# An encoder block with sixteen experts: weight tiles of neighbouring rows, token features permuted in their store, column tiles that stream runs of 32, and embedding inputs loaded ahead of the weights

## The chip, the cores and the metric

The kernel runs on one core of a Trainium2 chip. The metric is device time in microseconds (us); lower is better. Several runs of the kernel before were timed, and one further execution was recorded by the profiler. Engines are named as the profile names them: PE is TensorE (matmuls; PEld its weight loads), DVE VectorE, ACT ScalarE, POOL GpSimd, and SP the engine that issues most DMAs.

## The reference

Two requests, 256 and 512 tokens of 1024 features, pass through one block with shared weights: a mixer (dilated attention beside a bidirectional state space model), then a mixture of 16 experts in which each expert picks its tokens, then a gate that mixes in an embedding of each token. Everything is float32. The part that matters here:

```
aff = softmax(h @ w_router)                    # h: normed tokens (t, 1024); 16 experts
gate, idx = top_k(aff.T, 2 * t // 16)          # 64 tokens of 512, 32 of 256, per expert
ye = (silu(xe @ w_gate) * (xe @ w_up)) @ w_down   # xe = h[idx]; per expert 1024 -> 2816 -> 1024
out = zeros.at[idx].add(ye * gate)             # added back to the tokens' rows
...
e = rmsnorm(pe @ w_ple)                        # pe: an embedding input of 256 per token
x + sigmoid(rmsnorm(x) @ w_pg) * e
```

Each expert sees 96 tokens in all and has 34.6 MB of weights (w_gate and w_up 1024 x 2816, w_down 2816 x 1024), each of which is used once.

## The kernel before, in words

Up to the experts the block is worked off in a mixer part (projections, attention, state space), an output projection (`units_out`), and a router per 128 tokens (`router`, L770 on). The router squares and sums its rows, stores the updated rows to DRAM (`acc_d`, L782), scales the rows by the norm's gains on POOL (L786) and by the rstd on ACT (L787), and stores them to DRAM as `hn_d` (L788). `hn_d` and `acc_d` are laid out with four rows of 256 features for each token, its quarters j = 0 to 3. Then `top_k` finds each expert's tokens.

**Expert stage.** The 96 tokens are three blocks (b) of 32. `gather` (L1110 on) fetches for each block 128 rows of `hn_d`, so that partition 32j + token holds quarter j of that token. `turn_x` (L1116) turns such a block of 128 x 256 in squares of 32 x 32 on DVE, so that partition 32j + c has feature c of a group of 32 of quarter j, and the 32 tokens lie along the columns: a stationary operand of 128 x 32 for each of 8 contraction steps k. `blocks` (L1131) then runs, for each weight tile, 12 matmuls: for each block of tokens four column tiles j of 32 tokens, whose outputs go to partitions 32j to 32j + 31 of one PSUM bank. Column tile j streams a quarter of the weight tile's columns.

`up(e, r)` handles half r (1408) of the hidden features: 8 contraction steps, a gate tile and an up tile each; then ACT takes the silu, DVE the product and again a turn by squares of 32, which gives the stationary operands of `down(e, r)` with its 11 contraction steps. `emit` scales by the gates and adds the rows to `acc_d` by an indirect DMA. The order of the work is up(e, 0), down(e − 1, 1), emit(e − 1), up(e, 1), down(e, 0).

**Which row of a weight lies on which partition** is free so long as it agrees with the stationary operand. Before, a tile is loaded by `strips` (L203): 16 strips of 8 rows each, whose starts lie 1024/16 = 64 rows apart for gate and up, 1408/16 = 88 rows apart for down. Step k takes rows 8k to 8k + 7 of every strip. So quarter j's features must stand in the order (k, strip in the quarter, row) rather than (strip, k, row): `turn_x` has ACT copy each gathered block into `xp` with such a view (L1120, `by_strip` and `blocks32`), and the DVE product of the hidden features reads the same kind of view (L1151).

**The weights' stream.** `Feed` (L122) holds the list of all 864 expert tiles and the 8 tiles of w_pg that follow them. It has 22 slots of 5632 bytes per partition: 9 in the pool `w_b` (N_B), opened when attention's buffers are given back, 8 in `w_c` (N_C), 5 in `w_d` (N_D), opened when the embedding part's pool `ple` is given back. A slot that a tile's matmuls have finished with is loaded with the next tile. All these loads are issued by SP (L147), in the order of the list, in one queue with the other stores and loads of SP.

**The embedding part** runs beside the output projection. `ple_turn` (L825) takes the six blocks of tokens one after the other: it loads the input `pe` (128 x 256, two buffers; L829), and at a later step has PE transpose it and splits it into two parts for three-term matmuls. The first step of `ple_turn` is taken just ahead of `wf.add(w_b, N_B)` (L1058, L1059), so one `pe` load stands ahead of the first weights on SP, and the other five behind them.

Of the kernel before, what the change touches and what calls it, by code (L numbers as in the profile page):

```python
# [10 lines left out]
F32 = mybir.dt.float32  # L11
# [4 lines left out]
AF = mybir.ActivationFunctionType  # L16
ALU = mybir.AluOpType
# [4 lines left out]
P = 128  # L22
D = 1024
KD = D // P
NT = 6
# [8 lines left out]
NB = 3  # L34
FR = FF // 2
FC = FR // 4
DC = D // 4
KF = FR // P
PLE = 256
# [125 lines left out]
def block_kernel(ctx, tc, x_prompt, x_sample, p_prompt, p_sample, rel_bias, g_mix, w_in, conv_w, conv_b, dt_bias,  # L165
                 a_log, d_skip, g_ssd, w_out, g_ffn, w_router, w_gate, w_up, w_down, g_pg, w_pg, w_ple, g_ple,
                 g_final, c_masks, c_table, c_rows, y_prompt, y_sample):
    nc, E = tc.nc, mybir.EngineType
    S, Q = Group(0), Group(1)

    def rows(prompt, sample, t):
        return prompt[t * P:(t + 1) * P, :] if t < 2 else sample[(t - 2) * P:(t - 1) * P, :]

    x_rows = lambda t: rows(x_prompt[0], x_sample[0], t)
    p_rows = lambda t: rows(p_prompt[0, 0], p_sample[0, 0], t)
    N_B, N_C, N_D, PLE_A = 9, 8, 5, 4
    y_rows = lambda t: rows(y_prompt[0], y_sample[0], t)

    def row_bcast(v, n):
# [2 lines left out]
    def pool(name, side):  # L182
        return tc.alloc_tile_pool(name=name, bufs=1, side=side, reuse_waits="tile")
# [16 lines left out]
    items.append((w_ple[0].rearrange("(k p) c -> p k c", p=P), 2, D))  # L200
    ws = Stream(nc, items)

    def strips(w, r0, step, c0, n):  # L203

        w = w[r0:, c0:c0 + n]
        return bass.AP(tensor=w.tensor, offset=w.offset, ap=[[step * w.ap[0][0], 16], [w.ap[0][0], 8], [1, n]])

    def ups(e, r):
        return [strips(w[0, e], 8 * k, D // 16, FR * r, FR) for k in range(KD) for w in (w_gate, w_up)]

    def downs(e, r):
        return [strips(w_down[0, e], FR * r + 8 * k, FR // 16, 0, D) for k in range(KF)]

    def by_strip(ap):

        return ap.rearrange("p (q k v) -> p k q v", q=4, v=8)

    def blocks32(ap):
        return ap.rearrange("p (k q v) -> p k q v", q=4, v=8)

    order = []
    for e in range(NE):
        for r in range(2):
            order += ups(e, r) + (downs(e - 1 + r, 1 - r) if e + r else [])
# [10 lines left out]
    def bank(tag, bufs):  # L235
        return psum.tile([P, 512], F32, tag=tag, bufs=bufs, name=tag)

    pA = lambda: bank("pA", 2)
    pB = lambda: bank("pB", 3)
    pT = lambda: bank("pT", 2)  # L240
    pO = lambda: bank("pO", 1)
# [27 lines left out]
    def rstd_of(p, ss, n, width):  # L269
        r = p.tile([P, n], F32, tag="rstd", bufs=3, name="rstd")  # L270
        nc.vector.tensor_scalar(r, ss, 1.0 / width, EPS, op0=ALU.mult, op1=ALU.add)
        nc.gpsimd.tensor_tensor(r, r, mhalf[:, :n], op=ALU.pow)
        return r

    def sumsq(p, src, scr):
        ss = p.tile([P, 1], F32, tag="ss", bufs=3, name="ss")
        nc.scalar.activation(scr, src, AF.Square, accum_out=ss)
        return ss

    def transposes(src, k0, k, n=P, bank=None):  # L280
        p = (bank or pT)()
        for j in range(k):
            nc.tensor.transpose(p[:, j * n:(j + 1) * n], src[:, (k0 + j) * P:(k0 + j + 1) * P], ident[:n, :n])  # L283
        return p[:, :k * n].rearrange("p (j q) -> p j q", j=k)

    def split_to(hi, lo, src):
        nc.scalar.activation(hi, src, AF.Copy)  # L287
        nc.vector.tensor_tensor(lo, src, hi, op=ALU.subtract)
# [487 lines left out]
    def router(g, t, xm):  # L776

        row = slice(t * P, (t + 1) * P)
        hn = fin.tile([P, D], F32, tag="hn", bufs=2, name="hn")
        r = rstd_of(wk, sumsq(wk, xm, hn), 1, D)  # L780
        xT = fin.tile([P, KD, P], F32, tag="xT", bufs=2, name="xT")
        nc.sync.dma_start(g.acc_rows[row, :], xm)  # L782
        for k0 in (0, 4):
            src = transposes(xm, k0, 4)
            nc.scalar.activation(xT[:, k0:k0 + 4, :], src, AF.Copy)
        nc.gpsimd.tensor_tensor(hn, xm, gff, op=ALU.mult)  # L786
        nc.scalar.activation(hn, hn, AF.Copy, scale=r)  # L787
        nc.sync.dma_start(g.hn_rows[row, :], hn)  # L788
        yield
        pr = pB()  # L790
        for k in range(KD):
            nc.tensor.matmul(pr[:, :NE], lhsT=xT[:, k, :], rhs=wr[:, k, :], start=k == 0, stop=k == KD - 1)
        st = wk.tile([P, 4], F32, tag="st3", bufs=2, name="st3")
        af = wk.tile([P, NE], F32, tag="af", bufs=2, name="af")
        nc.vector.tensor_reduce(st[:, 0:1], pr[:, :NE], axis=AX.X, op=ALU.max)
        nc.vector.tensor_scalar(st[:, 1:2], st[:, 0:1], r, -1.0, op0=ALU.mult, op1=ALU.mult)
        nc.scalar.activation(af, pr[:, :NE], AF.Exp, bias=st[:, 1:2], scale=r, accum_out=st[:, 2:3])
        nc.vector.reciprocal(st[:, 3:4], st[:, 2:3])
        nc.vector.tensor_scalar(af, af, st[:, 3:4], None, op0=ALU.mult)
        yield  # L800
        p = pO()
        nc.tensor.transpose(p[:NE, :P], af, ident)
        nc.vector.tensor_copy(affs[0][g.row:g.row + NE, t * P:(t + 1) * P], p[:NE, :P])
        g.routed += 1
        yield
# [17 lines left out]
    evs, pts = {}, {}  # L823

    def ple_turn():  # L825

        for t in PLE_ORDER:
            pe = pw.tile([P, PLE], F32, tag="pe", bufs=2, name="pe")
            nc.sync.dma_start(pe, p_rows(t))  # L829
            yield  # L830
            pts[t] = [pw.tile([P, 2, P], F32R, name=f"pe{x}{t}") for x in "hl"]
            split_to(*pts[t], transposes(pe, 0, 2))
            yield

    def ple():
# [215 lines left out]
    gff = fin.tile([P, D], F32, name="gff")  # L1051
    nc.sync.dma_start(gff, row_bcast(g_ffn[0], D))
    w_b = pool("w_b", "right")
    pw = pool("ple", "right")
    PLE_ORDER = (2, 3, 4, 5, 0, 1)
# [30 lines left out]
    p, p_q = pO(), pB()  # L1086
# [19 lines left out]
    exw = pool("experts", "left")  # L1106
    of = (S, S, Q)
    xgs, xts, hts_, acc, pend = {}, {}, {}, {}, {}
# [7 lines left out]
    def turn_x(e):  # L1116
        xts[e] = [exw.tile([P, DC], F32, tag=f"x{b}", bufs=2, name="xe") for b in range(NB)]
        for b in range(NB):
            xp = exw.tile([P, DC], F32, tag="xp", bufs=2, name="xp")
            nc.scalar.activation(blocks32(xp), by_strip(xgs[e][b]), AF.Copy)  # L1120
            nc.vector.transpose(xts[e][b], xp)

    gather(0)
    wf.add(w_c, N_C)
# [1 line left out]
    w_d = pool("w_d", "right")  # L1126
    wf.add(w_d, N_D)
    turn_x(0)


    def blocks(out, st, k, w, n, first, last):  # L1131


        for b in range(NB):
            for j in range(4):
                q = slice(32 * j, 32 * j + 32)
                nc.tensor.matmul(out[b][q], lhsT=st[b][:, 32 * k:32 * k + 32], rhs=w[:, n * j:n * (j + 1)],  # L1137
                                 start=first[b], stop=last, skip_group_check=True)

    def up(e, r):  # L1140
        pg, pu = [pB()[:, :FC] for _ in range(NB)], [x()[:, :FC] for x in (pT, pT, pO)]
        for k in range(KD):
            for p in (pg, pu):
                i, w = wf.get()
                blocks(p, xts[e], k, w, FC, [k == 0] * NB, k == KD - 1)
                wf.free(i)
        hts_[e, r] = [exw.tile([P, FR // 4], F32, tag=f"h{b}", bufs=2, name="ht") for b in range(NB)]
        for b in range(NB):
            sg, hv = (exw.tile([P, FC], F32, tag=x, bufs=2, name=x) for x in ("sg", "hv"))
            nc.scalar.activation(sg, pg[b], AF.Silu)  # L1150
            nc.vector.tensor_tensor(blocks32(hv), by_strip(sg), by_strip(pu[b]), op=ALU.mult)  # L1151
            nc.vector.transpose(hts_[e, r][b], hv)  # L1152

    def down(e, r, after=None):
        if r == 0:
            two, one = pA(), pA()
            acc[e] = [two[:, :DC], two[:, DC:], one[:, :DC]]
        h = hts_.pop((e, r))
        for k in range(KF):
            i, w = wf.get()  # L1160
            first = r + k == 0
            blocks(acc[e], h, k, w, DC, [first, False, first], r == 1 and k == KF - 1)
            wf.free(i)
            if after:
                after()
# [12 lines left out]
    for e in range(NE):  # L1178
        if e + 1 < NE:
            gather(e + 1)  # L1180
        if 1 <= e <= NT:
            ple_norm(e - 1)
        for r in range(2):
            up(e, r)
            if r == 0 and e + 1 < NE:
                turn_x(e + 1)
            if e + r:
                down(e - 1 + r, 1 - r)
                if r == 0:
                    emit(e - 1)  # L1190
# [4 lines left out]
    def halve():  # L1195

        if len(wg) < KD and wf.n_dma == len(wf.items) and len(wf.slots) > 1:
# [3 lines left out]
            wf.slots.append(wf.held.pop(len(wf.items) - KD + i)[1])  # L1201

    down(NE - 1, 1, halve)
    emit(NE - 1)

# [22 lines left out]
    for t in range(NT):  # L1228
        if t + 1 < NT:
            tail_prep(t + 1)  # L1230
        xt, et, xh, xl, r = xs5.pop(t)
        sg = wf.tile(keep[1][t % 2], D)
        for c in range(2):
            s_ = slice(c * 512, (c + 1) * 512)
            p = pA()
# [5 lines left out]
        r = rstd_of(wk, sumsq(wk, sg, q5.tile([P, D], BF16, tag="scr5", bufs=1, name="scr5")), 1, D)  # L1241
# [64 lines left out]
```

## Time and profile before

| What | us |
| --- | --- |
| Median of three runs | 2746.53 (2706.67 to 2758.66) |
| The profiled execution, its own time | 2726.49 |
| Its span in the profile | 2724.6 |
| First expert matmul starts | 518.4 |
| Last expert matmul ends | 2616.0 |
| From there to the end | 108.6 |
| DMA moved, over the span | 642.07 MB |

How to read it: the profile is of one execution, and sums of parts have to be compared with its 2724.6 us span, which is 1.9 us less than its own time. In a group's row stand its line, engine, operation and operands, the number of instructions, their busy time, the mean duration of one, and the idle time of the engine ahead of them with what ended it. A float32 matmul appears as two records. The four column tiles of 32 run beside each other, so the records of one weight tile overlap, and a tile's time is read from the starts of successive tiles.

### The profile page before, as it was taken

What the parts mean: (1) busy time and instruction counts of PE and PEld (TensorE: products, weight loads), DVE (VectorE), ACT (ScalarE), POOL (GpSimd) and SP (SyncE); (2) the same over time, 40 slices, a digit from 0 to 9 for tenths busy, and PEclk for the clock granted to TensorE, in tenths of its full rate; (3) what the DMA queues carried; (4) which work ended last, traced back from release to release, by engine and by line L of the source; (5) the groups of instructions that cost most, each with busy time, mean ns of one, the idle gap of its engine ahead of it and who ended that gap; (6) DMA issues with size and microseconds to landing.
All of it is one profiled execution on the core that took longest, in us unless ns stands there. A gap on an engine that the chain in (4) does not pass through costs nothing.

```text
span 2724.6 us, 52864 instructions
## 1 busy us (share of the span) xinstructions
PE 2072.3 (76%) x23968; PEld 1073.0 (39%) x23968; DVE 476.4 (17%) x1001; ACT 417.8 (15%) x816; POOL 288.3 (11%) x279
## 2 busy tenths in 40 slices
PE   7999996797677767677777676766666777676758
PEld 6989895542222222222222222222222223222336
DVE  6675672400000000000000000000000000000024
ACT  5676363300000000000000000000000000000023
POOL 0343422200000000000001010101010000000000
PEclk9999998899999999999999999999999999999989
DMA  7441526999999999999999999999999999999952
GB/s 243 138 111 48 173 74 192 242 249 272 267 284 266 279 253 288 249 283 274 269 271 286 251 268 248 283 251 255 251 258 251 266 259 285 247 281 247 288 146 78
DMA packets 181743, 642.07 MB, mean 236 GB/s; under 512 B 21805, under 2 KB 56037, under 8 KB 181518
## 3 DMA queue, kind: packets, MB, share of 16 engines
q1 hardware_dynamic: 168318, 620.85, 85.9%
q0 software_dynamic: 13200, 17.84, 3.3%
q8 instruction: 188, 3.08, 0.5%
q14 instruction: 37, 0.30, 0.0%
HBM read 618.13 MB, written 19.96 MB: 234 GB/s over the span
## 4 chain that ended last, share of the span: by engine, by line
issue 73%; PE 13%; DMA 6%; POOL 4%; ACT 3%; DVE 2%; SPq 0%; POOLq 0%; DVEq 0%; ACTq 0%
PE pA L265 3%; PE pA L266 3%; PE pA L267 3%; DMA acc_d<-ye,quart 2%; POOL acc_d L1171 2%; PE pO L704 1%; POOL xg L1113 1%; DMA xg<-hn_d,quart 1%; DMA pe<-in_p_sample 1%; PE pT L695 1%; ACT ws L96 1%; DMA hn_d<-hn 1%; DMA ws<-in_w_in 1%; DVE ws L97 1%; PE pT L283 1%
## 5 line engine op out<-in xcount | busy, mean ns | idle before, releaser
L1137 PE MATMUL pB<-wf,xe 128*32 128x352 f32 x6144 | 517.1, 465 | 213.8 <-DMA wf<-in_w_gate 199.6
L1137 PE MATMUL pA<-wf,ht 128*32 128x256 f32 x8448 | 528.1, 384 | 177.2 <-DMA wf<-in_w_down 175.4
L1137 PE MATMUL pT<-wf,xe 128*32 128x352 f32 x4096 | 364.4, 466 | 181.8 <-DMA wf<-in_w_up 181.3
L1137 PEld LDWEIGHTS pA<-wf,ht 128*32 128x32 f32 x8448 | 245.2, 109 | 462.2 <-DMA wf<-in_w_down 330.7
L1137 PEld LDWEIGHTS pB<-wf,xe 128*32 128x32 f32 x6144 | 183.6, 110 | 533.9 <-DMA wf<-in_w_gate 293.9
L1151 DVE TENSOR_TENSOR hv<-sg,pT 128x352 f32<-128x352 f32 x64 | 32.1, 502 | 1942.7 <-PE pT L1137 1921.6
L1150 ACT ACTIVATE sg<-pB 128x352 f32<-128x352 f32 x96 | 44.6, 464 | 1619.1 <-PE pB L1137 1547.1
L1137 PEld LDWEIGHTS pT<-wf,xe 128*32 128x32 f32 x4096 | 114.6, 109 | 423.5 <-DMA wf<-in_w_up 292.7
L1171 POOL DMA_INDIRECT acc_d<-ye,quart x48 | 76.4, 1591 | 1563.6 <-ACT ye L1170 1447.4
L1137 PE MATMUL pO<-wf,xe 128*32 128x352 f32 x2048 | 204.9, 459 | 0.0
L1137 PEld LDWEIGHTS pO<-wf,xe 128*32 128x32 f32 x2048 | 70.5, 110 | 82.9 <-issue 70.4
L1113 POOL DMA_INDIRECT xg<-hn_d,quart x48 | 47.8, 996 | 446.9 <-ACT xp L1120 423.8
L97 DVE TENSOR_TENSOR ws<-ws 128x2048 fp32r<-128x2048 f32 (+1 forms) x31 | 69.4, 2241 | 40.3 <-ACT ws L96 40.3
L1170 ACT ACTIVATE ye<-pA,gates 128x256 f32<-128x256 f32 x48 | 19.4, 472 | 320.4 <-PE pA L1137 320.4
L96 ACT ACTIVATE ws<-ws 128x2048 fp32r<-128x2048 f32 (+1 forms) x31 | 55.9, 1806 | 29.7 <-PE pA L266 16.3
L265 PE MATMUL pA<-h,ws 128*128 128x512 f32 (+1 forms) x136 | 54.1, 398 | 0.0
L266 PE MATMUL pA<-h,ws 128*128 128x512 f32 (+1 forms) x136 | 53.8, 396 | 0.0
L267 PE MATMUL pA<-h,ws 128*128 128x512 f32 (+1 forms) x136 | 53.7, 395 | 0.0
L1152 DVE STREAM_TRANSPOSE ht<-hv 128x352 f32<-128x352 f32 x96 | 47.0, 515 | 0.6
L265 PE MATMUL pA<-hq,ws 128*128 128x256 f32 (+1 forms) x136 | 40.9, 302 | 4.7 <-ACT ws L96 4.1
L267 PE MATMUL pA<-hq,ws 128*128 128x256 f32 (+1 forms) x136 | 40.2, 297 | 1.3 <-DVE ws L97 1.3
L265 PE MATMUL pA<-ws,mh 128*128 128x512 f32 x96 | 38.8, 404 | 1.9 <-ACT mh L287 1.9
(302 smaller groups left out, 2048.9 us busy)
## 6 DMA issues: line engine op xcount, KB each, us to landing
wf<-in_w_gate SPq DMA_DIRECT2D x256, 704.0 KB
wf<-in_w_up SPq DMA_DIRECT2D x256, 704.0 KB
wf<-in_w_down SPq DMA_DIRECT2D x352, 512.0 KB
ws<-in_w_in SPq DMA_DIRECT2D x24, 1024.0 KB
tbl_rep<-tbl SPq DMA_DIRECT2D x8, 512.0 KB
ws<-in_w_out SPq DMA_DIRECT2D x4, 1024.0 KB
wf<-in_w_pg SPq DMA_DIRECT2D x8, 512.0 KB
sk<-tbl_rep SPq DMA_DIRECT2D x8, 448.0 KB
```

Source lines behind the costliest of these rows:

```text
L96: self.nc.scalar.activation(hi, raw, AF.Copy)
L97: self.nc.vector.tensor_tensor(lo, raw, hi, op=ALU.subtract)
L265: nc.tensor.matmul(out, lhsT=sh, rhs=mh, start=first, stop=False)
L266: nc.tensor.matmul(out, lhsT=sh, rhs=ml, start=False, stop=False)
L267: nc.tensor.matmul(out, lhsT=sl, rhs=mh, start=False, stop=last)
L283: nc.tensor.transpose(p[:, j * n:(j + 1) * n], src[:, (k0 + j) * P:(k0 + j + 1) * P], ident[:n, :n])
L1113: nc.gpsimd.indirect_dma_start(out=xgs[e][b], out_offset=None, in_=of[b].hn_d, in_offset=bass.IndirectOffsetOnAxis(ap=quart[:, b, e:e + 1] ...
L1137: nc.tensor.matmul(out[b][q], lhsT=st[b][:, 32 * k:32 * k + 32], rhs=w[:, n * j:n * (j + 1)], start=first[b], stop=last, skip_group_check= ...
L1150: nc.scalar.activation(sg, pg[b], AF.Silu)
L1151: nc.vector.tensor_tensor(blocks32(hv), by_strip(sg), by_strip(pu[b]), op=ALU.mult)
L1152: nc.vector.transpose(hts_[e, r][b], hv)
L1171: nc.gpsimd.indirect_dma_start(out=of[b].acc_d, out_offset=bass.IndirectOffsetOnAxis(ap=quart[:, b, e:e + 1], axis=0), in_=ye, in_offset=N ...
```

## The change

Three things are changed together.

1. *Rows that neighbour.* A weight tile is now 128 rows that follow each other. `strips`, `by_strip` and `blocks32` are gone.
2. *The orders that go with it.* Contraction step k of `up` needs features 128k + 32j + c on partition 32j + c. The router's POOL product therefore writes `hn` permuted, quarter j made of the 32-feature runs j of every 128 (`by_tile`), and `turn_x` turns the gathered block at once, without the ACT copy. Column tile j of a gate or up tile streams the runs j of 32 columns of every 128 (11 runs of 32 instead of 352 columns in a row), so that after the turn the hidden features stand in the order in which w_down's rows lie; the DVE product reads and writes in a row. Column tiles of w_down still stream 256 columns in a row.
3. *Embedding inputs.* All six `pe` loads are issued at the first step of `ple_turn`, each to a buffer of its own; the transposes follow in later steps. The pool `ple` is larger for that, and N_B, N_C, N_D are 8, 8, 6 instead of 9, 8, 5.

```
-    N_B, N_C, N_D, PLE_A = 9, 8, 5, 4
+    N_B, N_C, N_D, PLE_A = 8, 8, 6, 4
...
     def ups(e, r):
-        return [strips(w[0, e], 8 * k, D // 16, FR * r, FR) for k in range(KD) for w in (w_gate, w_up)]
+        return [w[0, e, P * k:P * (k + 1), FR * r:FR * (r + 1)] for k in range(KD) for w in (w_gate, w_up)]
 
     def downs(e, r):
-        return [strips(w_down[0, e], FR * r + 8 * k, FR // 16, 0, D) for k in range(KF)]
+        return [w_down[0, e, FR * r + P * k:FR * r + P * (k + 1), :] for k in range(KF)]
...
+    def by_tile(ap):
+
+        return ap.rearrange("p (k j c) -> p j k c", j=4, c=32)
...
-        nc.gpsimd.tensor_tensor(hn, xm, gff, op=ALU.mult)
+        nc.gpsimd.tensor_tensor(hn.rearrange("p (j k c) -> p j k c", j=4, c=32), by_tile(xm), by_tile(gff), op=ALU.mult)
...
+        pes = [pw.tile([P, PLE], F32, name=f"pe{t}") for t in range(NT)]
         for t in PLE_ORDER:
-            pe = pw.tile([P, PLE], F32, tag="pe", bufs=2, name="pe")
-            nc.sync.dma_start(pe, p_rows(t))
-            yield
+            nc.sync.dma_start(pes[t], p_rows(t))
+        yield
+        for t in PLE_ORDER:
             pts[t] = [pw.tile([P, 2, P], F32R, name=f"pe{x}{t}") for x in "hl"]
-            split_to(*pts[t], transposes(pe, 0, 2))
+            split_to(*pts[t], transposes(pes[t], 0, 2))
             yield
...
-            xp = exw.tile([P, DC], F32, tag="xp", bufs=2, name="xp")
-            nc.scalar.activation(blocks32(xp), by_strip(xgs[e][b]), AF.Copy)
-            nc.vector.transpose(xts[e][b], xp)
+            nc.vector.transpose(xts[e][b], xgs[e][b])
...
-                q = slice(32 * j, 32 * j + 32)
-                nc.tensor.matmul(out[b][q], lhsT=st[b][:, 32 * k:32 * k + 32], rhs=w[:, n * j:n * (j + 1)],
+                nc.tensor.matmul(out[b][32 * j:32 * j + 32], lhsT=st[b][:, 32 * k:32 * k + 32], rhs=w[:, j],
...
-                blocks(p, xts[e], k, w, FC, [k == 0] * NB, k == KD - 1)
+                blocks([x.rearrange("p (k c) -> p k c", c=32) for x in p], xts[e], k, by_tile(w), [k == 0] * NB, k == KD - 1)
...
-            nc.vector.tensor_tensor(blocks32(hv), by_strip(sg), by_strip(pu[b]), op=ALU.mult)
+            nc.vector.tensor_tensor(hv, sg, pu[b], op=ALU.mult)
...
-            blocks(acc[e], h, k, w, DC, [first, False, first], r == 1 and k == KF - 1)
+            blocks(acc[e], h, k, w.rearrange("p (j c) -> p j c", j=4), [first, False, first], r == 1 and k == KF - 1)
```

What moves on SP, at the place where the weights' stream begins (`pe` are the embedding inputs, `wf` the weight slots, `gff` the router's gains, `acc_d` and `hn_d` the router's stores). Before:

```order
L1052 DMA gff<-in_g_ffn 128x1024
L829 DMA pe<-in_p_sample 128x256
L147 DMA wf<-in_w_gate 128x1x1408
L147 DMA wf<-in_w_up 128x1x1408
...
L147 DMA wf<-in_w_gate 128x1x1408
L829 DMA pe<-in_p_sample 128x256 x2
L1176 DMA g<-in_g_ple 128x1024
L782 DMA acc_d_85<-xm 128x1024 x2
L788 DMA hn_d_84<-hn 128x1024 x2
L829 DMA pe<-in_p_sample 128x256
L829 DMA pe<-in_p_prompt 128x256 x2
```

and with the change:

```order
L1045 DMA gff<-in_g_ffn 128x1024
L821 DMA pe_4234<-in_p_sample 128x256
L821 DMA pe_4235<-in_p_sample 128x256
...
L821 DMA pe_4233<-in_p_prompt 128x256
L147 DMA wf<-in_w_gate 128x1408
L147 DMA wf<-in_w_up 128x1408
...
L147 DMA wf<-in_w_up 128x1408
L1166 DMA g<-in_g_ple 128x1024
L774 DMA acc_d_85<-xm 128x1024
L780 DMA hn_d_84<-hn 128x1024
```

Five `pe` loads have moved from behind the nine weight tiles of `w_b` to ahead of its eight. On ACT, where the expert stage begins, before:

```order
L277 ACTIVATE scr,ss<-ev 128x1024 x6
L1120 ACTIVATE xp<-xg 128x256 x8
L1150 ACT_TABLE_LOAD
L1150 ACTIVATE sg<-pB 128x352 x6
L1120 ACTIVATE xp<-xg 128x256 x3
L1150 ACTIVATE sg<-pB 128x352 x3
```

and with the change:

```order
L1140 ACTIVATE sg<-pB 128x352 x9
L1160 ACTIVATE ye<-pA,gates 128x256 x3
L1140 ACTIVATE sg<-pB 128x352 x6
```

The copies of gathered blocks (`xg` to `xp`) are gone; the silu steps (`sg`) follow each other, with only the scaling of the outputs (`ye`) between them.

More of the change, by code (lines that the diff above doesn't have):

```diff
@@ L201, in block_kernel @@
     ws = Stream(nc, items)
-    def strips(w, r0, step, c0, n):
-        w = w[r0:, c0:c0 + n]
-        return bass.AP(tensor=w.tensor, offset=w.offset, ap=[[step * w.ap[0][0], 16], [w.ap[0][0], 8], [1, n]])
     def ups(e, r):
-        return [strips(w[0, e], 8 * k, D // 16, FR * r, FR) for k in range(KD) for w in (w_gate, w_up)]
+        return [w[0, e, P * k:P * (k + 1), FR * r:FR * (r + 1)] for k in range(KD) for w in (w_gate, w_up)]
     def downs(e, r):
-        return [strips(w_down[0, e], FR * r + 8 * k, FR // 16, 0, D) for k in range(KF)]
[L214 to L219, printed above, removed]
+        return [w_down[0, e, FR * r + P * k:FR * r + P * (k + 1), :] for k in range(KF)]
+    def by_tile(ap):
+        return ap.rearrange("p (k j c) -> p j k c", j=4, c=32)
     order = []
@@ L1128, in block_kernel, with blocks @@
     turn_x(0)
-    def blocks(out, st, k, w, n, first, last):
+    def blocks(out, st, k, w, first, last):
         for b in range(NB):
             for j in range(4):
-                q = slice(32 * j, 32 * j + 32)
-                nc.tensor.matmul(out[b][q], lhsT=st[b][:, 32 * k:32 * k + 32], rhs=w[:, n * j:n * (j + 1)],
+                nc.tensor.matmul(out[b][32 * j:32 * j + 32], lhsT=st[b][:, 32 * k:32 * k + 32], rhs=w[:, j],
                                  start=first[b], stop=last, skip_group_check=True)
     def up(e, r):
-        pg, pu = [pB()[:, :FC] for _ in range(NB)], [x()[:, :FC] for x in (pT, pT, pO)]
+        pg, pu = ([x()[:, :FC] for x in xs] for xs in ((pB, pB, pB), (pT, pT, pO)))
         for k in range(KD):
```

## The prediction

> **What bounds the kernel now.** I read the windows by stage first. Columns: stretch, length, then for each engine its busy time (x instructions), then TensorE's granted clock, the busy share of the 16 DMA engines, GB/s.
>
> ```profile
> 400.00:460.00 60.00, 39.97 (x237) 33.85 (x236) 16.73 (x37) 17.35 (x29) 8.71 (x6) 0.86 0.69 184
> 460.00:500.00 40.00, 38.90 (x236) 33.14 (x235) 23.96 (x70) 19.61 (x40) 8.70 (x6) 1.00 0.72 200
> ...
> 2616.00:2724.60 108.60, 75.15 (x340) 60.08 (x336) 50.17 (x74) 38.37 (x60) 11.76 (x15) 0.86 0.23 77
> ```
>
> and the stretch from the first expert matmul to the last:
>
> ```profile
> 518.35:2616.00 2097.65, 1538.40 (x20736) 608.34 (x20736) 104.42 (x240) 81.97 (x189) 114.95 (x90) 1.00 1.03 265
> ```
>
> The experts take 2097.65 of 2724.6 us. In that stretch TensorE is busy for 73%, at full clock; the DMA engines never rest (1.03), yet bring only 265 GB/s. What the profile's groups say of the idle time agrees:
>
> ```profile
> L1137 PE MATMUL pB<-wf,xe 128*32 128x352 f32 x6144 | 517.1, 465 | 213.8 <-DMA wf<-in_w_gate 199.6
> L1137 PE MATMUL pA<-wf,ht 128*32 128x256 f32 x8448 | 528.1, 384 | 177.2 <-DMA wf<-in_w_down 175.4
> L1137 PE MATMUL pT<-wf,xe 128*32 128x352 f32 x4096 | 364.4, 466 | 181.8 <-DMA wf<-in_w_up 181.3
> ```
>
> 556 us of waiting, all for weights. By the DMA issues each gate or up tile is 704.0 KB (512 of them), each down tile 512.0 KB (352): 553.65 MB, which at 265 GB/s is 2089 us. So the stage is its transfers, and its rate is the question. Next I looked for other loads in the same trace. The last eight tiles of this queue are w_pg's: 128 rows that lie one behind the other, 4 KB each. The DMA view from 2600 to 2630 us, in 40 slices of 0.75 us (share in tenths, then GB/s):
>
> ```profile
> DMA  9999899999999999998999975543432000000000
> GB/s 213 257 240 268 235 229 240 262 251 229 224 235 240 224 235 218 251 273 213 399 404 404 393 284 208 213 175 158 164 137 93 33 0 0 0 0 0 0 0 0
> ```
>
> Up to the 19th slice the strips of w_down come, in packets of the same 4 KB, at 213 to 273 GB/s. Then, with the engines as busy as before, 399, 404, 404: w_pg. (Afterwards some engines have finished and the share falls.) Same queue, same packet, same destination, only other rows: the strips cost a third of the bandwidth. **I take 400 GB/s for rows that neighbour.**
>
> **Part 1, the experts' rows.** A strip tile reads 16 places, each 8 rows: 64 rows apart for gate and up (704 KB), 88 for down (352 KB). The new one reads 128 rows in a row; the bytes, packets' length, number of DMAs and their order stay. Before the matmuls begin, the 16 tiles of the first two pools can be loaded (11.5 MB); 542.1 MB remain: at 400 GB/s 1355 us. Beside them run the gathers and scatter-adds; in 1000 to 1140 us, about one expert, their queue took:
>
> ```profile
> q0 software_dynamic: 576, 0.79, 3.0%
> ```
>
> 3.0% of 140 us is 4.2 us per expert with the strips in the way; I take 3, so 48 us for 16. The stream then needs 1403 us.
>
> Now TensorE becomes the neighbour to watch. While tiles were in stock, its own pace shows in the timeline, one gate and one up tile (48 records) from row to row, and a run of 11 down tiles:
>
> ```profile
> 531.50 1.98 PE L1137 MATMUL pB<-wf,xe 128*32 128x352 f32 x24
> ...
> 535.05 1.98 PE L1137 MATMUL pB<-wf,xe 128*32 128x352 f32 x24
> ...
> 538.61 1.98 PE L1137 MATMUL pB<-wf,xe 128*32 128x352 f32 x24
> ...
> 577.65 0.42 PE L1137 MATMUL pA<-wf,ht 128*32 128x256 f32 x3
> ...
> 578.09 14.18 PE L1137 MATMUL pA<-wf,ht 128*32 128x256 f32 x256
> ```
>
> 7.11 us for two pairs: 1.777 us per gate or up tile (400 GB/s bring one in 1.80). Down: 264 records in about 14.4 us, 1.31 us per tile (1.31 by the DMA). An expert has 32 and 22: 56.9 + 28.8 = 85.7 us, 1371 us for 16. The two limits nearly meet; the stream is the longer by 32 us. Since neither covers the other's jitter, I add 13 us: **the stage takes 1416 us instead of 2098.**
>
> **Part 2, the strided moving operand.** A gate or up matmul now streams 11 runs of 32 columns, 128 apart, instead of 352 in a row; 8 blocks of 32 tokens and the PSUM side stay as they were. Time goes by columns: 1777 ns / 24 records / 352 columns is 0.210 ns, 1310 / 24 / 256 is 0.213, so nothing can be gained by it. What it could cost, the trace bounds only from afar: L494 streams runs of 8, L792 16 columns in a row.
>
> ```profile
> L792 PE MATMUL pB<-wr,xT 128*128 128x16 f32 x96 | 11.4, 256 | 0.2 <-ACT xT L785 0.2
> ...
> L499 PE MATMUL pB<-masks,ad 128*128 128x128 f32 x24 | 3.3, 274 | 0.0
> ...
> L494 PE MATMUL pB<-dt,masks 128*128 128x32 f32 x12 | 1.5, 274 | 0.0
> ```
>
> Runs of 8 take 274 ns, as 128 columns in a row do, and 7% over the shortest. So 0 to 7%; I take 0, since 32-column runs are nearer to a plain row. 7% would make an up tile 1.90 us and an expert 89.6, 1434 us in all, still inside the sum's slack. [...]
>
> **Part 3, the permuted store.** Six POOL products at L786 (2.4 us each) read permuted views. A POOL product with spread-out operands is L616, 1286 ns for 512 columns against 2400 for 1024:
>
> ```profile
> L786 POOL TENSOR_TENSOR hn<-xm,gff x6: 2340/2400/2411, 420.6 to 488.2; 128x1024 f32<-128x1024 f32 x6
> ```
>
> ```profile
> L616 POOL TENSOR_TENSOR w<-gt,dt 128x512 f32<-128x512 f32 x24 | 30.2, 1286 | 22.1 <-DVE gt L571 20.6 <-DVE e L619 1.6
> ```
>
> That is 0 to 0.2 us on the path, once; nothing in the sum. In return 48 ACT copies of 417 ns go; 47 lie under the weights' stream, where ACT is busy 4%, and one is ahead of the first expert matmul: −0.4 us. VectorE's products lose their strided reads; they too lie under the stream.
>
> **Part 4, the head.** Now only the first embedding tile is issued ahead of nine weights; TensorE's queue has the second one's transpose in front of other work and stands:
>
> ```profile
> 441.42 0.66 PE L283 MATMUL pT<-masks,pe 128*128 128x128 f32 x2 [17.86 <-DMA pe<-in_p_sample]
> ```
>
> With all six ahead of the weights this wait goes, −17.9 us. On SP's queue the six stand where the first one stood, behind its wait for the end of attention; the weights behind them waited for that before, too. [...]
>
> ```profile
> 492.35 14.91 DMA hn_d<-hn
> ...
> 508.02 16.55 DMA xg<-hn_d,quart x2
> ```
>
> ```profile
> 518.35 1.40 PE L1137 MATMUL pB<-wf,xe 128*32 128x352 f32 x8 [13.47 <-DVE xe L1121]
> ```
>
> The store stands behind weights on SP's queue: 14.91 x (1 − 265/400) = −5.0; a gather (9.1 us from issue to landing) by the same ratio −3. The six loads delay the weights by 0.79 MB, 2 to 3 us, hidden by the slack of 460 to 500 (share 0.72); of the 22 slots one opens later (w_b 8, w_d 6), hidden by the 16 tiles, 28 us of TensorE's work; without that cover, 1.8 us. The first expert matmul moves from 518.4 to **492.1**.
>
> **The sum**, for the profiled execution (2726.5 = 518.4 + 2097.6 + 108.6 + 1.9 outside the span): 492.1 + 1416 + 108.6 + 1.9 = 2019. The tail is not touched. The runs shown have their median 0.7% above the profiled one; I add 6 us for that: **2025 us**. Its own range is 1970 (TensorE alone sets the stage: 1371 + 603) to 2110 (375 GB/s: 1446 + 61 + 603).
>
> **Rivals.** (a) *The long rows don't reach 400.* w_pg's 512 KB lie in one piece; gate and up take halves of 11 KB rows, 64% of the bytes of an expert. Two stretches of ordinary loads while TensorE works, most of their packets 1 to 4 KB:
>
> ```profile
> 28.00:36.00 8.00, 6.74 (x59) 6.03 (x57) 5.82 (x8) 6.44 (x7) 0.00 (x0) 1.00 0.95 313
> 300.00:350.00 50.00, 49.39 (x227) 40.21 (x226) 23.98 (x49) 22.79 (x40) 21.03 (x27) 1.00 0.65 203
> ```
>
> 313 / 0.95 = 329 and 203 / 0.65 = 312 GB/s at full share; by the lower 492 + 1737 + 61 + 111 = 2401. Halfway, at 356, the stage takes 1523 + 61 = 1584 and the run 2187. For it: only 3 us of w_pg at full rate. Against: those early loads have the shorter packets. [...]
>
> (b) *The rows' place isn't the cause.* w_pg came last, with TensorE idle; if a running TensorE slows the transfers, the stage stays at 265 and only the head's 26 us are won: 2700, no change by the 2% that a measurement of this kernel can tell. Against it: in the two stretches under (a) TensorE worked for 84% and 99% of the time, beside loads that ran at 329 and 312 GB/s.
>
> (c) *TensorE pays for the runs.* If the strided stream costs a fifth, an expert takes 97.1 us and the run 2156. It would have to cost 83% (3.24 us per tile: 2124 us for the stage eat the head's gain) to make the kernel slower; at double, 142.5 us per expert, the run takes 2281 + 603 = 2884. For it: the trace has no such stream. Against: the runs of 8 above.
>
> **Chances.** Forecast 0.74, (a) 0.12, (b) 0.04, (c) 0.10, of which 0.04 slow enough to be slower than before. So faster by over 2%: 0.74 + 0.12 + 0.06 = 0.92; within 2%: 0.04; slower: 0.04. For 8 in 10 the range takes the forecast's own and the nearer half of (a) and of the mild (c): 1970 to 2180.
>
> **What would show it.** Right: the stage's window at 380 GB/s or more, TensorE busy for over 90% of it and waits for wf under 100 us in all; expert matmul records still 459 ns and 74 ns apart where tiles are in stock; no wait for pe; first expert matmul near 492. Wrong: a window at 265 (b) or 310 to 360 (a) with DMA share 1.03; or records farther apart than 74 ns with the DMA share falling below 1, SP then waiting for TensorE (c).

## The result, and the profile after

The changed kernel takes 1994.57 us (median of four runs, 1989.97 to 1999.15) against 2737.32 us, a ratio of 0.7314 with a 95% interval of 0.7244 to 0.7384. Forecast were 2025 us, 1970 to 2180. The profiled execution took 1995.17 us with a span of 1993.4 us.

The top of its page: busy time of the engines, then the span in 40 slices.

```profile
PE 1910.5 (96%) x23968; PEld 1224.0 (61%) x23968; DVE 476.6 (24%) x1001; ACT 398.2 (20%) x768; POOL 286.8 (14%) x279
...
PE   6999999997999999999999999999999999999778
...
DMA  8544116356899999999999999999999999999921
GB/s 262 161 130 115 50 63 195 101 227 264 324 410 405 411 403 405 403 400 408 396 412 400 399 407 398 408 401 401 408 399 409 399 406 402 407 404 399 357 72 64
```

Before, these three rows were:

```profile
PE   7999996797677767677777676766666777676758
...
DMA  7441526999999999999999999999999999999952
GB/s 243 138 111 48 173 74 192 242 249 272 267 284 266 279 253 288 249 283 274 269 271 286 251 268 248 283 251 255 251 258 251 266 259 285 247 281 247 288 146 78
```

In the expert stage TensorE's row is now 9 from end to end where it was 6 or 7 from the 13th slice on, and the DMA engines, at a share of 1.02 against 1.03, bring about 404 GB/s instead of 247 to 288. The stage's window, from the first to the last expert matmul (same columns as before: length, busy time of the engines, clock, DMA share, GB/s):

```profile
497.87:1883.70 1385.83, 1377.43 (x20736) 759.09 (x20736) 103.33 (x239) 63.22 (x142) 115.17 (x90) 1.00 1.02 401
```

1385.8 us instead of 2097.7; TensorE is busy for 99.4% of it. The groups that held 556 us of waits for weights now stand like this:

```profile
L1127 PE MATMUL pB<-wf,xe 128*32 128x352 f32 x6144 | 589.7, 461 | 15.9 <-DVE xe L1112 12.7
L1127 PE MATMUL pA<-wf,ht 128*32 128x256 f32 x8448 | 473.3, 379 | 1.0 <-DMA wf<-in_w_down 0.9
L1127 PE MATMUL pT<-wf,xe 128*32 128x352 f32 x4096 | 437.3, 461 | 4.2 <-DMA wf<-in_w_up 4.0
```

Of these groups' idle time 12.7 us stand ahead of the first matmul; 8 us are left beside them, most of it for weights. While tiles are in stock the timeline shows the same pace as before, 3.55 us for a gate and an up tile (rows between them left out):

```profile
507.72 1.98 PE L1127 MATMUL pB<-wf,xe 128*32 128x352 f32 x24
...
511.27 1.98 PE L1127 MATMUL pB<-wf,xe 128*32 128x352 f32 x24
...
514.82 1.98 PE L1127 MATMUL pB<-wf,xe 128*32 128x352 f32 x24
```

So runs of 32 columns cost TensorE nothing that shows in these 3.55 us. In all: 497.9 us to the first expert matmul, 1385.8 for the stage, 109.7 behind it and 1.8 outside the span, 1995.2 us.

### The profile page after: what moved, and what is told of

The parts are those of the page before. It is cut to its first block, busy times and chain, and to the rows that moved or that the text cites. A ratio compares the mean times of both kernels' runs of the same rounds, so it can differ in the third digit from the quotient of the medians.

```text
span 1993.4 us, 52814 instructions
## 1 busy us (share of the span) xinstructions
PE 1910.5 (96%) x23968; PEld 1224.0 (61%) x23968; DVE 476.6 (24%) x1001; ACT 398.2 (20%) x768; POOL 286.8 (14%) x279
## 5 line engine op out<-in xcount | busy, mean ns | idle before, releaser
L1127 PE MATMUL pB<-wf,xe 128*32 128x352 f32 x6144 | 589.7, 461 | 15.9 <-DVE xe L1112 12.7
L1127 PE MATMUL pA<-wf,ht 128*32 128x256 f32 x8448 | 473.3, 379 | 1.0 <-DMA wf<-in_w_down 0.9
L1127 PE MATMUL pT<-wf,xe 128*32 128x352 f32 x4096 | 437.3, 461 | 4.2 <-DMA wf<-in_w_up 4.0
L1127 PEld LDWEIGHTS pA<-wf,ht 128*32 128x32 f32 x8448 | 313.4, 110 | 157.6 <-DMA wf<-in_w_down 8.4
L1127 PEld LDWEIGHTS pB<-wf,xe 128*32 128x32 f32 x6144 | 253.2, 110 | 241.7 <-issue 55.2
L1127 PE MATMUL pO<-wf,xe 128*32 128x352 f32 x2048 | 282.6, 459 | 0.0
L1127 PEld LDWEIGHTS pT<-wf,xe 128*32 128x32 f32 x4096 | 175.7, 110 | 164.0 <-issue 35.7
L1127 PEld LDWEIGHTS pO<-wf,xe 128*32 128x32 f32 x2048 | 103.2, 110 | 75.8 <-issue 24.9
L264 POOL TENSOR_TENSOR rstd<-rstd,mhalf 128x1 f32<-128x1 f32 (+1 forms) x36 | 23.6, 658 | 152.4 <-DVE rstd L263 150.7
```

What stands on the lines that cost most here:

```text
L1127: nc.tensor.matmul(out[b][32 * j:32 * j + 32], lhsT=st[b][:, 32 * k:32 * k + 32], rhs=w[:, j], start=first[b], stop=last, skip_group_check ...
```

## The experiments

Their diffs are against the changed kernel, unless another is named. First, what is each part worth, and which limit sets the stage; then why strips were slow; last, what a strided moving operand costs.

### Rows without the embedding part, and the embedding part without the rows

`rows_alone`, the changed kernel with the old loads:

```
-    N_B, N_C, N_D, PLE_A = 8, 8, 6, 4
+    N_B, N_C, N_D, PLE_A = 9, 8, 5, 4
...
-            nc.sync.dma_start(pes[t], p_rows(t))
+            pe = pw.tile([P, PLE], F32, tag="pe", bufs=2, name="pe")
+            nc.sync.dma_start(pe, p_rows(t))
+            yield
```

> The change without its third part: neighbouring rows and the new orders, but the embedding inputs loaded one by one behind nine weight tiles, as before. If the head's gain is the pe wait at full size (17.9 us), this runs 18 to 20 us above the change: about 2014 us. If the faster stream also drains the weights ahead of pe sooner, the wait shrinks to 17.9 x 265/400, about 12 us or less, and the run is about 2005 us. The expert stage stays at 1386 us by both.

Measured: 2005.61 us, ratio 0.7465 (0.7444 to 0.7487). The change itself took 1996.35 us beside it, so part 3 is worth 9 us here; the first expert matmul starts at 507.9 us, against 499.9 in that run of the change. The wait for `pe` did shrink by itself, even more than by the ratio of the rates, from 17.9 to 5.6 us:

```profile
L275 PE MATMUL pT<-masks,pe 128*128 128x128 f32 x12 | 2.6, 302 | 5.6 <-DMA pe<-in_p_sample 5.6
```

`pe_alone` is the opposite: the kernel before with the new loads and slots (the third part of the diff shown above, nothing else).

> The kernel before with the third part alone: strips stay, all six embedding inputs are loaded ahead of the weights. By the prediction's step the wait of 17.9 us goes and the first expert matmul moves to about 500 us; the stage stays at 2098 us and 265 GB/s, the run is 18 to 20 us below before, ratio 0.993. Rival: since the stream alone sets the stage, an earlier start is eaten by it, the stage grows by as much and the ratio is 1.000.

Measured: 2732.68 us against 2737.3 us, both medians. Of single runs before took 2686 to 2781 us, this one 2718 to 2752: a gain or loss of 20 us, 0.7%, would not stand out of that, so the times decide between neither expectation. The trace does for the head: the wait for `pe` is gone, but the first expert matmul comes at 512.8 us, 5.6 us earlier than before, not 18. The chain of waits and the timeline tell what took over:

```profile
479.44 22.26 DMA hn_d<-hn
```

```profile
501.77 1.06 ACT L277 ACTIVATE scr<-ev 128x1024 bf16<-128x1024 f32 x1 [9.10 <-DMA hn_d<-hn]
...
508.73 0.70 ACT L1121 ACTIVATE xp<-xg 128x256 f32<-128x256 f32 x2
...
512.78 1.40 PE L1138 MATMUL pB<-wf,xe 128*32 128x352 f32 x8 [19.18 <-DVE xe L1122]
```

The last store of `hn` lands 22.26 us after its issue, where it took 14.91: it is issued 13 us earlier and stands in the queue of the slow weights. ACT waits for it with the embedding norms (L277), which stand ahead of the copies of the first gathered tokens (L1121) on that engine. So with the slow stream the wait moved from one transfer behind the weights to the next.

### What holds the first expert matmul

`after_again` is the change itself, run beside the next kernel.

> The change itself, on the same chip as the next kernel: 1995 us, ratio 0.73.

It took 1996.35 us, ratio 0.7428 (0.7412 to 0.7444). In the change's own trace the six norms of the embeddings (L846) stand on DVE between the gathers (485.0 us, 5.7 us to landing) and the first turn of gathered tokens:

```profile
489.32 3.67 DVE L846 SCALAR_TENSOR_TENSOR ev<-ev,rstd,g 128x1024 f32<-128x1024 f32 x3 [1.49 <-DMA wf<-in_w_gate]
...
493.79 3.68 DVE L846 SCALAR_TENSOR_TENSOR ev<-ev,rstd,g 128x1024 f32<-128x1024 f32 x3 [0.53 <-POOL rstd L264]
497.38 1.09 DVE L1112 STREAM_TRANSPOSE xe<-xg 128x256 f32<-128x256 f32 x3
```

`norms_late` makes them wait for the first hidden features:

```
+            if e + r == 0:
+                scr = exw.tile([P, D], BF16, tag="scr", bufs=1, name="scr")
+                nc.vector.tensor_copy(scr[:, :1], hts_[0, 0][0][:, :1])
             if r == 0 and e + 1 < NE:
                 turn_x(e + 1)
```

> The change, with the six embedding norms held back until the first hidden features exist (one DVE copy of one column into the norms' scratch tile does that). If the norms on ACT and DVE are what holds the first transpose of gathered tokens, and so the first expert matmul (497.9 us), it starts 4 to 6 us earlier, at about 493 us, and as TensorE sets the stage the run ends 4 to 6 us earlier, 1990 us. Rival: the gather's landing holds it, and nothing moves; or the stream sets the stage, the start moves and the end does not.

```profile
491.93 1.40 PE L1127 MATMUL pB<-wf,xe 128*32 128x352 f32 x8 [6.25 <-DVE xe L1112]
```

The first matmul starts at 491.9 us (499.9 in `after_again`), and the run takes 1992.01 us, ratio 0.7408 (0.7386 to 0.7430): 4.3 us less, all six runs (1985.85 to 1993.52) below all six of the change (1994.01 to 1998.01). The norms were what held it. Of the kernels that do all of the block's work this was the fastest, by these 4 us; half of the earlier start is lost again.

### Which limit sets the stage

`two_blocks` takes work from TensorE and leaves the stream as it is:

```
         for b in range(NB):
+            if b == 1 and not (first[0] or last):
+                continue
             for j in range(4):
```

> The change, with one of the three blocks of tokens given only its first and last contraction steps (the output of that block is left incomplete). TensorE's work per expert falls from 85.7 to about 63 us, so the stream alone sets the stage. If TensorE was the bound by its own 1371 us and the stream close behind, the stage falls from 1386 us to the stream's time, 542 MB at 404 GB/s, about 1345 us, and the run takes about 1955 us. If the stream was the bound already, the stage stays at 1386 us.

```profile
497.00:1870.00 1373.00, 1152.40 (x15104) 473.89 (x15104) 103.45 (x240) 63.97 (x143) 115.18 (x90) 0.99 1.02 404
```

1972.15 us. With TensorE at 84% and the DMA engines at full share, this stage of 1373 us is the stream's own time. TensorE's own is 1371 us by the pace of its tiles. Together they take 1386. So neither of the expected cases is it: the two limits are equal within 0.2%, and 13 us are lost where they meet. Less work for TensorE alone was worth these 13 us; a faster stream alone, which no run tries, could by TensorE's pace be worth 15 at most. (The run is 24 us shorter than `after_again`; the rest lies in the tail, 100 us here, for which this kernel was not made and which was not followed up.)

### Why the strips were slow

The prediction put it down to rows that lie apart. Five kernels change only which rows a tile takes, and in which form the access is written. The first keeps the strips with uneven distances:

```
+        return [strips(w[0, e], 8 * k, 63, FR * r, FR) for k in range(KD) for w in (w_gate, w_up)]
...
+        return [strips(w_down[0, e], FR * r + 8 * k, 87, 0, D) for k in range(KF)]
```

> The change, with each weight tile read as 16 places of 8 rows again, but 63 rows apart for gate and up and 87 for down, instead of 64 and 88 (the weights thus stand on partitions that do not agree with the tokens, and some rows are read twice: the output is another one, the work is the same). If it was the even distance (704 KB and 352 KB, multiples of 64 and 32 KB) that made strips slow, 693 KB and 348 KB bring the rate back: 390 GB/s or more, about 2000 us. If it is the distance itself, the rate stays at 265 GB/s and the run takes about 2700 us.

Measured: 2719.43 us (eight runs, 2697 to 2743), with 268 GB/s from 600 to 1800 us: the even distance is not it. The next brings the down strips close together, `strips(w_down[0, e], FR * r + 8 * k, 16, 0, D)`:

> The change, with only the down tiles read as 16 places of 8 rows, 16 rows (64 KB) apart, over a region of 1 MB (other rows than the tokens agree with, so another output). If distance makes strips slow, these near places run at 400 GB/s and the run takes about 1995 us. If an even distance of 64 KB does, the down runs fall to about 240 GB/s: 22 x 0.524 MB x 16 at 240 instead of 404 is 312 us more, about 2300 us.

Measured: 2491.43 us. The DMA view of 100 us of the stage, in slices of 2.5 us:

```profile
DMA  9999999999999999999999999999999999999999
GB/s 236 228 223 237 249 256 266 386 417 417 410 419 412 405 424 317 230 218 221 242 213 249 251 243 285 283 240 252 249 301 385 415 421 362 358 388 423 348 416 246
```

The rate swings between 220 and 250 GB/s and 410 to 420: down tiles from near places are as slow as from far ones (213 to 273 GB/s in the prediction's view). The slices below 310 GB/s move 13.5 MB, and the 15 down tiles issued in this window hold 7.9 MB, so gate and up tiles in flight beside them seem to be slow too. At this point both theories, distance and even distance, had trouble: one says that near strips are fast, the other that 63 rows are. What the slow kernels have in common is the form: an access of three levels, 16 groups x 8 rows x the row. w_pg, which the prediction took for comparison, differs from strips in that too: it is written as 128 rows x the row. The next two kernels separate the two properties. `rows_apart` takes far rows in the plain form:

```
-        return [w[0, e, P * k:P * (k + 1), FR * r:FR * (r + 1)] for k in range(KD) for w in (w_gate, w_up)]
+        return [w[0, e].rearrange("(p k) c -> k p c", p=P)[k, :, FR * r:FR * (r + 1)] for k in range(KD) for w in (w_gate, w_up)]
...
+        return [w_down[0, e, FR * r:FR * (r + 1), :].rearrange("(p k) c -> k p c", p=P)[k] for k in range(KF)]
```

> The change, with the 128 rows of a tile taken far from each other by one even step: every eighth row for gate and up (88 KB apart, a region of 11.5 MB), every eleventh for down (44 KB apart), written as 128 rows of one length (the weights do not agree with the tokens' order, so another output). If it is the rows' distance that made strips slow, as the prediction had it, the stream falls to about 265 GB/s and the run takes about 2700 us. If it is the form of the access, 16 groups of 8 rows in place of 128 rows, it stays at 404 GB/s and 1995 us.

and `strips_9` takes near rows in the form of strips: `strips(w[0, e], 120 * k, 9, FR * r, FR)` and `strips(w_down[0, e], FR * r + 120 * k, 9, 0, D)`.

> The change, with each tile read in the form of the strips, 16 groups of 8 rows, but with the groups only 9 rows apart, so that all rows lie within 144 (one row in nine is left out: another output). Distance: 128 rows of 144 are neighbours, 400 GB/s, about 1995 us. Form: 265 GB/s, about 2700 us, as with groups 64 or 63 rows apart.

`strips_32` splits the rows in two levels as well, but as 32 groups of 4:

```
-        return bass.AP(tensor=w.tensor, offset=w.offset, ap=[[step * w.ap[0][0], 16], [w.ap[0][0], 8], [1, n]])
+        return bass.AP(tensor=w.tensor, offset=w.offset, ap=[[step * w.ap[0][0], 32], [w.ap[0][0], 4], [1, n]])
```

> As the last, but with 32 groups of 4 rows, 5 rows apart. If only the split of the rows in two levels counts, the rate is again about 265 GB/s (2700 us). If it counts how the 128 partitions fall to the 16 DMA engines, 8 in a row to each with 16 groups, another split can give another rate, up to 404 GB/s (1995 us).

The windows from 600 to 1800 us of the kernel before, the change, `rows_apart`, `strips_9` and `strips_32`, in this order:

```profile
600.00:1800.00 1200.00, 875.31 (x11740) 338.71 (x11732) 58.04 (x135) 46.31 (x108) 69.57 (x54) 1.00 1.03 270
```

```profile
600.00:1800.00 1200.00, 1192.32 (x18006) 661.66 (x18002) 89.17 (x207) 54.94 (x124) 101.94 (x78) 1.00 1.02 404
```

```profile
600.00:1800.00 1200.00, 1190.68 (x17994) 663.61 (x17990) 89.42 (x207) 55.34 (x126) 101.95 (x78) 1.00 1.02 404
```

```profile
600.00:1800.00 1200.00, 873.92 (x11724) 339.26 (x11728) 58.05 (x135) 35.91 (x81) 69.48 (x54) 1.00 1.03 269
```

```profile
600.00:1800.00 1200.00, 1191.41 (x17991) 664.71 (x17987) 87.79 (x204) 54.37 (x123) 101.96 (x78) 1.00 1.02 404
```

| Kernel | Rows of a tile | Form | us | GB/s |
| --- | --- | --- | --- | --- |
| the change | neighbours | 128 rows | 1995 | 404 |
| `rows_apart` | 88 and 44 KB apart | 128 rows | 1996 | 404 |
| `strips_32` | 160 rows, one in five left out | 32 groups x 4 rows | 1993 | 404 |
| `strips_9` | 144 rows, one in nine left out | 16 groups x 8 rows | 2723 | 269 |
| before | groups 704 and 352 KB apart | 16 groups x 8 rows | 2737 | 270 |

This settles what decides the rate: at the distances tried, where the rows lie changes nothing for 16 x 8 or for 128 rows, and neither does a split in two levels as such. 16 groups of 8 cost a third of the bandwidth (269 and 270 GB/s against 404). Why is not shown. The number 16 is that of the DMA engines in the profile, so a group may be one engine's share; this is a guess from the count alone, it leaves open why 32 groups of 4 are fast, and no trace here names the engine of a packet. Why near down strips cost as much as 495 us more than the change also stays open.

### What a strided moving operand costs

`runs_of_1` and `runs_of_2` give gate and up column tiles of shorter runs:

```
-                blocks([x.rearrange("p (k c) -> p k c", c=32) for x in p], xts[e], k, by_tile(w), [k == 0] * NB, k == KD - 1)
+                blocks(p, xts[e], k, w.rearrange("p (c j) -> p j c", j=4), [k == 0] * NB, k == KD - 1)
```

> The change, with column tile j of gate and up streaming every fourth column instead of runs of 32 (hidden features then stand in another order than the rows of the down weights, so another output). If a moving operand costs by its columns alone, an up tile stays at 1.777 us and the run at 1995 us. If single float32 values 16 bytes apart cost TensorE a second access each, up to twice: 3.55 us per tile, 142 us per expert, about 2890 us.

```profile
516.79 3.96 PE L1127 MATMUL pB<-wf,xe 128*32 128x352 f32 x24
...
524.23 3.96 PE L1127 MATMUL pB<-wf,xe 128*32 128x352 f32 x24
```

2982.37 us, ratio 1.0898 (1.0722 to 1.1075): slower than the kernel before. A pair of tiles takes 7.44 us instead of 3.55, 2.1 times as long. With `w.rearrange("p (k j c) -> p j k c", j=4, c=2)`:

> The change, with column tiles of gate and up streaming runs of 2 columns, 8 apart, instead of runs of 32, 128 apart (another order of hidden features, so another output). Single columns 16 bytes apart cost 800 ns a record against 459. [...]

```profile
506.61 2.10 PE L1127 MATMUL pB<-wf,xe 128*32 128x352 f32 x24
...
510.39 2.11 PE L1127 MATMUL pB<-wf,xe 128*32 128x352 f32 x24
```

2026.43 us; 3.78 us for a pair, 6.5% more than the 3.55 us of runs of 32, and far from the 7.44 us of single columns. A record lasts 478 ns, where single columns take 803 and runs of 32 461. So the traces of the three put the price at 2.1 times for one column, 1.065 for two and 1.00 for 32, with a small price left at two.

## Why the prediction was right, and where it was not

**The stream's rate (part 1): the number right, the cause wrong.** 400 GB/s were taken, 404 came. But the step "Same queue, same packet, same destination, only other rows" failed: w_pg differed from the strips in the form of its access as well, and it is the form that counts (`rows_apart` 404 GB/s, `strips_9` 269). The rate came out right by luck: the change altered place and form at once. None of the rivals named this: (a) and (b) both asked only where rows lie or what else runs. A change that made neighbouring rows in the old form would have been forecast at 2025 us, and `strips_9` shows what it gives: 2723.

**The stream's length was over-sized by 30 us.** 1355 us at 400 GB/s plus 48 us for gathers and scatter-adds gave 1403; alone it takes 1373 (`two_blocks`). The window's 404 GB/s are weights and small transfers together; 542.1 MB of weights and 12.6 MB of gathered and added rows (96 transfers of 128 KB) at that rate are 1373 us, so the small ones cost 31 us by their bytes and rate, not 48, and the weights' own 1355 were 13 too long.

**TensorE's pace and the meeting of the limits held.** 1371 us, 13 us of friction: the stage took 1386, which is 1373 and 13. By the sum, 1416 were forecast, and the difference of 30 us is the stream's. The prediction had the stream longer by 32 us, where 2 are measured. Two figures beside the sum are off: gate and up tiles are two thirds of an expert's bytes, not 64%, and the 1434 us for a 7% dearer operand exceed the 1416 that they were said to fit.

**The strided operand (part 2): right.** 0 of 0 to 7% was taken; 3.55 us per pair. Rival (c) had its mechanism right and its place wrong: single columns do cost more than double (2982 us, above its 2884), runs of 32 nothing.

**The head (part 4) was over-sized by 6 us, and one of its steps failed.** Forecast 492.1, found 497.9. The wait for `pe` went. But "a gather by the same ratio" and the store of `hn` were not what came next: the gathers land after 5.7 us instead of 9.1, and the turn of the tokens then waits for the norms on DVE (`norms_late`). That the gathers stand in one queue with the weights, as the store of `hn` does, no run shows: from 1000 to 1140 us of the kernel before, q0 moved 0.79 MB, as much as three gathers and three scatter-adds of 128 KB hold, beside 36.79 MB in q1. That the 17.9 us are a gain of their own is also not so: with strips the store takes over and 5.6 us are left at the head, and no gain that stands out of the runs' scatter (`pe_alone`); with the fast stream the wait was down to 5.6 us by itself, and part 3 brings 9 us.

**The tail** was taken as untouched: 109.7 us against 108.6. The 6 us added for a median above the profiled run were not there: the median is 1994.57 us, the profiled run 1995.17. So the forecast lies 30 us too high: 30 from the stage and 6 of this allowance, less 6 from the head and 1 from the tail.

**Rival (b)**, a stream that stays at 265 GB/s, is what one would have had with the old form, wherever the rows lie. Its heading, that the place isn't the cause, was true; its reason was not, for 404 GB/s came beside a TensorE that was busy for 99% of the time.

## What to carry to other kernels

When a transfer is compared with a slower one in the same trace, list everything in which the two accesses differ, the levels of the pattern among them; a test that changes one of them at a time costs a line. Here a load from 16 groups x 8 rows ran at 269 GB/s, 128 rows or 32 groups x 4 rows at 404; near and far rows were alike in the two forms tried with both, 16 x 8 and 128 rows. Once the stage's two limits stand at 1371 and 1373 us and it takes 1386, only work that shortens both, or the head and the tail, can be worth more than about 15 us.

## What the runs showed of the hardware that was not expected

- The form of the source decided a load's rate at the same bytes and share of the DMA engines: 16 x 8 rows of 5.6 and 4 KB bring 269 GB/s, 32 x 4 bring 404, with the DMA engines at a share of 1.03 and 1.02 (`strips_9`, `strips_32`).
- Rows 44 and 88 KB apart load as fast as rows in one piece: 404 GB/s (`rows_apart` and the change).
- A float32 moving operand (128 x 352 in four column tiles) of single columns 16 bytes apart takes 2.1 times as long (`runs_of_1`, 7.44 us a pair of tiles), of pairs 32 bytes apart 1.065 times (`runs_of_2`, 3.78), of runs of 32 no longer than a plain row (3.55 in the change and before).
